# Grouped MoE on one core: the conditional of the rare pass moves from the second pair to the first, its loads change queue, and a nested conditional is taken out of its parent

## The chip, the core and the metric

The kernel runs on one core of a Trainium2 chip. The metric is the time of one execution on the device in microseconds (us), the median of several runs. TensorE (PE in the profile) multiplies matrices, ScalarE (ACT) evaluates functions, VectorE (DVE) does elementwise work, GpSimd (POOL) a little, and SyncE (SP) issues the loads. Each engine runs its own list of instructions in order and waits for others by semaphores.

## What is computed

The reference is a hybrid block followed by a two-layer block, 256 tokens of width 1024, in float32. The change lies in the second one:

```python
for l in range(2):
    h = rmsnorm(x, norm1_g[l]) * (1.0 + sc1) + sh1
    x = x + g1 * token_mix(h, ...)          # HGRN2 and latent attention
    h = rmsnorm(x, norm2_g[l]) * (1.0 + sc2) + sh2
    x = x + g2 * grouped_moe(h, w_router, router_bias, w_gate[l], w_up[l], w_down[l])
...
for e in range(N_EXPERTS):                  # in grouped_moe: 16 experts, top 2 of one group
    he = jax.nn.silu(t @ w_gate[e]) * (t @ w_up[e])
    y = y + combine[:, e:e + 1] * (he @ w_down[e])
```

A token goes to two experts, so `combine` is mostly zero, and the kernel computes an expert for its own tokens only. How many these are is known at run time alone.

## The kernel before

**Loads.** All weights are read as pages of 1 MB ([128, 2048] in float32) in the order of a list, PLAN. `pump` (L322) issues the next loads as long as a buffer is free, all from SyncE's queue (L346); `get` hands a page out and `release` (L377) gives buffers back and calls `pump`. Since SyncE's list is in order, a load issued behind something that waits, waits with it. In the MoE a pair of experts takes 12 pages (8 of gate and up, 4 of down), and 16 buffers are there. In layer 0 w166 is the first load that needs a buffer of pair 0; w174 to w181 hold gate and up of pair 2, w182 to w185 its down weights.

**The MoE** (`moe`, L1757) works on eight pairs of experts. Two pairs are fixed, the other six are sorted by load, so that their pages are found by indices in registers. For each pair: `gate_up` of slots 0 to 31 of both experts (L1593, 32 groups of matmuls over four blocks of partitions); `more_gate_up` (L1633), which holds a conditional for slots 32 to 63 (`If(cv > 32)`, L1637) and inside it, for the pairs with a limit of 96, one for slots 64 to 95 (`If(cv > 64)`, L1650); the release of 8 pages; the part of the previous pair's scatter for slots over 64 (L1773); `slot_w` (L1521), which sums the slots' weights; the scatter of the previous pair back to the tokens in two halves (L1532, L1533); `swiglu` (L1601 transposes, L1605 Silu on ScalarE, L1606 product on VectorE); and `downs` (L1657), which multiplies by the down weights (L1615) and copies the result (L1541, L1542). After every second pair `gather` (L1474) fetches the tokens of the next two pairs by a one-hot matmul (L1483), which ScalarE and VectorE copy into page tiles (L1490, L1492); the same pool of page tiles, from `self.page()`, serves several users. The next `gate_up` reads these tiles.

**The rare pass** (`rest`, L1744) computes what doesn't fit the limits: an outer conditional on the largest load, `If(top > NORMAL)` (L1749, NORMAL is 96), and in it sixteen inner ones (L1753) around `rare` (L1681). In this input no expert has over 96 tokens, so the outer one is skipped in both layers. Its body stands in the lists of four engines (PE, ACT, DVE, SP). `RARE_AT` names the pair at which it is placed, behind that pair's `swiglu`. The loads of `rare` fill page tiles from SyncE's queue (L1708).

**Order.** The instructions are placed on each engine by a scheduler that follows priorities; `issue_after` holds what is in it behind a named instruction. An `If` becomes a branch on every engine named. On an engine that skips it, a short row of instructions stands behind the branch, which waits for and adds to semaphores so that the counts are as if the body had run.

Of the kernel before, what the change touches and what calls it, by code (L numbers as in the profile page):

```python
# [11 lines left out]
F32 = mybir.dt.float32  # L12
# [3 lines left out]
AF = mybir.ActivationFunctionType  # L16
ALU = mybir.AluOpType
AX = mybir.AxisListType
ENG = mybir.EngineType

P = 128
S = 256
D = 1024
# [4 lines left out]
NPAIR = 8  # L28
# [184 lines left out]
FIXED = 2  # L213
NDYN = NPAIR - FIXED
# [1 line left out]
LIMITS = tuple([96] * FIXED + [96 if r < 3 else 64 for r in RANKS])  # L216
NORMAL = 96
HALF = 64
RARE_AT = 1
LEVELS = (64, 32, 16, 8, 4, 2, 1, 0)  # L220


# [52 lines left out]
class K:  # L275
# [71 lines left out]
            self.tiles[i] = t  # L347
            self.owner[i] = own

    def weight(self, i):  # L350
        if i not in self.dyn:
            return self.d["w"][i]
        return self.d["w"][bass.ds(self.dyn[i], 1)].rearrange("a p c -> p (a c)")

    def extra(self, pool, n, keys, cut=0):
        i = self.taken
# [1276 lines left out]
    def more_gate_up(self, p, cv, gu, x1, tg, h2, pw):  # L1633
        nc, tc = self.nc, self.tc
        ox = self.rt.tile([P, 2, S], F32, name=self.uid("ox"), tag="ox")
        more = LIMITS[p] > HALF
        with tc.If(cv > 32):  # L1637
            if more:
                xs = self.over_pick(p, 64)
            ps = self.mm()  # L1640
            last = self.gate_up(ps, gu, x1, range(4))
            if more:
                last = self.chain(last, self.over_turn(xs, ox))
            self.weigh(pw, p, 0, 1)
            last = self.gate_up(ps, gu, x1, range(4, 8), last)
            nc.scalar.activation(tg, ps, AF.Copy)
            if not more:
                return
            with tc.issue_after(last.ins):
                with tc.If(cv > 64):  # L1650
                    ps = self.mm()
                    self.gate_up(ps, gu, lambda k, e: ox[:, k // 4, (k % 4) * 64 + 32 * e:(k % 4) * 64 + 32 * e + 32])
                    t2 = self.sq512()
                    nc.scalar.activation(t2, ps, AF.Copy)
                    self.swiglu(t2, h2)

    def downs(self, p, cv, dn, hT, y, w, more):  # L1657
        nc, tc = self.nc, self.tc
# [22 lines left out]
    def rare(self, p, e, lo, w0):  # L1681
        nc = self.nc
        v = nc.vector
        c = [tt * 16 + 2 * p + e for tt in range(2)]
        pos = self.small(2)
        for tt in range(2):
            src = self.posm[:, c[tt]:c[tt] + 1]
            v.scalar_tensor_tensor(pos[:, tt:tt + 1], src, float(lo), src, ALU.is_gt, ALU.mult)
        o = min(lo, P)
        io = self.co("iota")[:, o:o + P]  # L1690
        pm = self.tmp.tile([P, 2, P], F32R, name=self.uid("pm"), tag="t1")
        for tt in range(2):
            v.tensor_scalar(pm[:, tt], io, pos[:, tt:tt + 1], None, ALU.is_equal)
        xo = []
        for h in range(2):
            ps = self.pick(pm, h)
            xs = self.sq512()
            nc.scalar.activation(xs, ps, AF.Copy)
            pt = self.acc()
            for i in range(4):  # L1700
                nc.tensor.transpose(pt[:, i * P:(i + 1) * P], xs[:, i * P:(i + 1) * P], self.ident)
            x = self.sq512()
            self.modulated(x[:, :], pt[:, :].rearrange("p (k s) -> p k s", k=4), h, P)
            xo.append(x)

        def load(i, half):
            t = self.page()
            nc.sync.dma_start(out=t, in_=self.weight(w0 + 12 * p + i)[:, half * 1024:(half + 1) * 1024])  # L1708
            return t

        gps = [self.acc() for _ in range(2)]
        for h in range(2):
            for u in range(2):
                for half in range(2):
                    t = load(4 * h + 2 * u + e, half)
                    for k2 in range(2):
                        k = 2 * half + k2
                        nc.tensor.matmul(gps[u], lhsT=xo[h][:, k * P:(k + 1) * P], rhs=t[:, k2 * 512:(k2 + 1) * 512],
                                         start=(h == 0 and k == 0), stop=(h == 1 and k == 3))
        sg = self.sq512()  # L1720
        nc.scalar.activation(sg, gps[0], AF.Silu)
        v.tensor_tensor(sg, sg, gps[1], ALU.mult)
        pt = self.acc()
        for f in range(4):
            nc.tensor.transpose(pt[:, f * P:(f + 1) * P], sg[:, f * P:(f + 1) * P], self.ident)
        hT = self.sq512()
        nc.scalar.activation(hT, pt, AF.Copy)
        pw = self.tmp.tile([P, 2, P], F32, name=self.uid("pw"), tag="t1")
        for tt in range(2):
            v.tensor_scalar(pw[:, tt], io, pos[:, tt:tt + 1], self.comb[:, c[tt]:c[tt] + 1], ALU.is_equal, ALU.mult)  # L1730
        w, st = self.slots()
        self.slot_w(pw, w, st)
        pss = [self.acc() for _ in range(2)]
        for f in range(4):
            t = load(8 + 2 * (f // 2) + e, f % 2)
            for n in range(2):
                nc.tensor.matmul(pss[n], lhsT=hT[:, f * P:(f + 1) * P], rhs=t[:, n * 512:(n + 1) * 512],
                                 start=(f == 0), stop=(f == 3))
        for n in range(2):
            yh, yl = self.sq512(F32R), self.sq512(F32R)  # L1740
            self.y_out(yh, yl, pss[n], w)
            self.scatter(yh, yl, st, 4 * n, 4)

    def rest(self, w0):  # L1744
        engs = [ENG.PE, ENG.Activation, ENG.DVE, ENG.SP]
        load = lambda i: self.count(i, engs)
        top = self.nc.values_load(self.srti[0:1, 2 * NDYN:2 * NDYN + 1], engines=engs, min_val=0,
                                  max_val=S + NORMAL - HALF)
        with self.tc.If(top > NORMAL):  # L1749
            for p in range(NPAIR):  # L1750
                cv = load(p)
                for lo in (LIMITS[p], LIMITS[p] + P):
                    with self.tc.If(cv > lo):  # L1753
                        for e in range(2):
                            self.rare(p, e, lo, w0)

    def moe(self, l, ahead):  # L1757
# [7 lines left out]
        tg = [self.rt.tile([P, 512], F32, name=self.uid("tg"), tag=f"tg{i}") for i in range(2)]  # L1765
        nc.gpsimd.memset(tg[1], 0.0)
        xe = self.gather(self.pm0)
        prev = cvp = None
        more = [self.rt.tile([P, D], F32R, name=self.uid("y2"), tag=f"y2{i}") for i in range(2)]
        more += self.slots("st2")  # L1770
# [5 lines left out]
        for p in range(NPAIR):  # L1776
            base = (p % 2) * P
            pw = self.rt.tile([P, 2, P], F32, name=self.uid("pw"), tag="pw")
            self.weigh(pw, p, 0)
            gu = [[[self.get(nm) for _ in range(2)] for nm in ("w_gate_2", "w_up_2")] for _ in range(2)]  # L1780
            x = lambda lvl: lambda k, e: xe[k // 4][:, (k % 4) * S + base + 64 * e + 32 * lvl:
                                                    (k % 4) * S + base + 64 * e + 32 * lvl + 32]
            hT = [self.rt.tile([P, S], F32, name=self.uid("hT"), tag=f"hT{i}") for i in range(3)]
            ps = self.mm()
            last = self.gate_up(ps, gu, x(0))
            nc.scalar.activation(tg[0], ps, AF.Copy)
            cv = self.count(p, engs)
            with self.tc.issue_after(last.ins):
                self.more_gate_up(p, cv, gu, x(1), tg[1], hT[2], pw)
            gu = None  # L1790
            self.release(8)
            if p > 0 and LIMITS[p - 1] > HALF:
                more_scatter()
            w, st = self.slots("sT", 2)
            self.slot_w(pw, w, st)
            last = None
            if prev is not None:
                self.scatter(*prev, 0, 4)
            for i in range(2):
                self.swiglu(tg[i], hT[i])  # L1800
            if p == RARE_AT:
                self.rest(w0)
            if prev is not None:
                last = self.scatter(*prev, 4, 4, 512)
            if p % 2 == 1 and p < NPAIR - 1:
                xe = self.gather(self.onehot(p // 2 + 1)[0])
            dn = [[self.get("w_down_2") for _ in range(2)] for _ in range(2)]
            if p == NPAIR - 1:
                ahead()
            y = [self.pga.tile([P, D], F32R, name=self.uid("pg"), tag="pg") for _ in range(2)]  # L1810
            with ExitStack() as after:
                if last is not None:
                    after.enter_context(self.tc.issue_after(last.ins))
                self.downs(p, cv, dn, hT, y, w, more)
            prev, cvp = (y[0], y[1], st), cv
            dn = None
            self.release(4)
# [213 lines left out]
```

## Time and profile before

| | before |
|---|---|
| median of 3 runs | 1503.02 us (1501.43 to 1504.09) |
| profiled execution | 1502.92 us |
| its span in the trace | 1501.1 us |
| mean granted clock of TensorE | 0.959 |
| TensorE busy | 1367.6 us (91%) |
| VectorE busy | 969.4 us (65%) |
| ScalarE busy | 680.7 us (45%) |
| read and written in device memory | 401.7 MB, 268 GB/s over the span |

The span is the time from the first to the last instruction that the trace holds; the execution's own time is 1.8 us longer. The two token mixes of the second block stand at 505 to 738 and 996 to 1229 us, the two MoEs behind them. In the rows of the trace, the us in brackets are the time that the engine sat idle before that group, and the name behind the arrow is what ended it. A name with a q (PEq, SPq) stands for an engine's sequencer, which takes branches, semaphores and the issue of transfers. "PEld" is the load of a matmul's stationary operand.

### The profile page before, as it was taken

The page shows a single profiled execution, that of the slowest core. Times are in us where ns is not written, and L with a number is a line of the kernel's source. Part 1 is how long each engine was busy: PE and PEld are TensorE (multiplying, and loading weights), DVE is VectorE, ACT ScalarE, POOL GpSimd, SP SyncE. Part 2 cuts the span into 40 slices and gives each one's busy share as a digit, 9 for nine tenths or more (in the row PEclk, how much of TensorE's full clock was granted, in tenths as well). Part 3 has the DMA queues.
Part 4 walks back from the last instruction along what each step waited for, and adds up shares of the span by engine and source line. Part 5 has one row for each costly group of instructions (what it writes and reads, how often), then busy time and mean ns, then how long its engine had stood idle before and what let it go on. Part 6 is the DMA issues. An engine that isn't in the chain of part 4 may idle for free. (4 is left out here: it accounts for less than half of the span.)

```text
span 1501.1 us, 27480 instructions
## 1 busy us (share of the span) xinstructions
PE 1367.6 (91%) x10654; PEld 1090.7 (73%) x10654; DVE 969.4 (65%) x2157; ACT 680.7 (45%) x1464; POOL 72.6 (5%) x86
## 2 busy tenths in 40 slices
PE   7999999989999999999856899988999986689988
PEld 7999998879999987999723344368789982334424
DVE  7999677888888788986621334368888762133323
ACT  7565458665556577555311112247756532011212
POOL 2010000010000003000100000000200010000010
PEclk9999999999999999999987999999999998799998
DMA  9787425368787143496687789963339678868895
GB/s 377 307 326 296 156 100 177 131 273 331 293 332 275 45 147 122 191 383 219 274 362 315 311 363 379 421 244 128 141 155 379 232 301 325 352 270 350 346 420 214
DMA packets 56904, 403.99 MB, mean 269 GB/s; under 512 B 6432, under 2 KB 6560, under 8 KB 8992
## 3 DMA queue, kind: packets, MB, share of 16 engines
q1 hardware_dynamic: 56736, 401.74, 67.6%
q8 instruction: 107, 1.75, 0.5%
q14 instruction: 61, 0.50, 0.1%
HBM read 400.66 MB, written 1.05 MB: 268 GB/s over the span
## 5 line engine op out<-in xcount | busy, mean ns | idle before, releaser
L389 ACT ACTIVATE whi<-w 128x512 fp32r<-128x512 f32 (+3 forms) x438 | 309.0, 737 | 242.7 <-PE mm L407 143.3
L390 DVE TENSOR_TENSOR wlo<-w,whi 128x512 fp32r<-128x512 f32 (+3 forms) x438 | 354.4, 829 | 62.0 <-ACT whi L389 60.4
L406 PE MATMUL mm<-nh,whi 128*128 128x256 f32 x1312 | 373.4, 285 | 14.3 <-ACT whi L389 13.5
L408 PE MATMUL mm<-nh,wlo 128*128 128x256 f32 x1312 | 370.8, 283 | 4.8 <-DVE wlo L390 4.8
L407 PE MATMUL mm<-nl,whi 128*128 128x256 f32 x1312 | 370.1, 282 | 0.3 <-DVE nl L529 0.2
L406 PEld LDWEIGHTS mm<-nh,whi 128*128 128x128 f32 x1312 | 249.7, 190 | 16.6 <-ACT whi L389 14.1
L408 PEld LDWEIGHTS mm<-nh,wlo 128*128 128x128 f32 x1312 | 249.2, 190 | 7.1 <-DVE wlo L390 6.5
L407 PEld LDWEIGHTS mm<-nl,whi 128*128 128x128 f32 x1312 | 249.8, 190 | 1.8 <-DVE nl L529 0.7
L1593 PE MATMUL mm<-w,pg 128*32 128x512 f32 x1472 | 184.5, 616 | 27.2 <-ACT pg L1490 19.6
L1593 PEld LDWEIGHTS mm<-w,pg 128*32 128x32 f32 x1472 | 51.1, 113 | 145.8 <-issue 104.6
L499 DVE SCALAR_TENSOR_TENSOR ada<-w,cact,ada 128x512 f32<-128x512 f32 x168 | 128.3, 763 | 6.5 <-ACT ada L496 3.6
L406 PE MATMUL acc<-hh,whi 128*128 128x256 f32 x352 | 98.9, 283 | 1.0 <-ACT whi L389 1.0
L407 PE MATMUL acc<-hl,whi 128*128 128x256 f32 x352 | 99.1, 282 | 0.0
L408 PE MATMUL acc<-hh,wlo 128*128 128x256 f32 x352 | 99.1, 283 | 0.0
L1536 DVE SCALAR_TENSOR_TENSOR xTt<-acc,mod,xTt 128x256 f32<-128x256 f32 x152 | 64.1, 475 | 38.2 <-PE acc L1533 38.0
L406 PEld LDWEIGHTS acc<-hh,whi 128*128 128x128 f32 x352 | 66.8, 190 | 1.1 <-ACT whi L389 1.1
L407 PEld LDWEIGHTS acc<-hl,whi 128*128 128x128 f32 x352 | 67.0, 190 | 0.0
L408 PEld LDWEIGHTS acc<-hh,wlo 128*128 128x128 f32 x352 | 67.0, 191 | 0.0
L1542 DVE SCALAR_TENSOR_TENSOR pg<-mm,sm,pg 128x512 fp32r<-128x512 f32 x32 | 23.8, 750 | 57.7 <-ACT pg L1541 46.6
L407 PE MATMUL mm<-wlo,nh 128*128 128x512 f32 (+2 forms) x144 | 54.8, 381 | 5.1 <-DVE wlo L390 5.1
L1510 DVE TENSOR_TENSOR pw<-cot,posp 128x128 f32<-128x128 f32 x52 | 12.9, 286 | 70.3 <-PE acc L1521 70.2
L1490 ACT ACTIVATE pg<-acc,mod,sm 128x256 f32<-128x256 f32 x32 | 17.4, 564 | 87.3 <-SPq L1749 60.1
(424 smaller groups left out, 2334.5 us busy)
## 6 DMA issues: line engine op xcount, KB each, us to landing
w<-in_w_dram SPq DMA_DIRECT2D x371, 1024.0 KB, 8.7
w<-in_w_dram SPq DMA_DIRECT2D x4, 832.0 KB, 8.3
w<-in_w_dram SPq DMA_DIRECT2D x4, 576.0 KB, 3.7
xTt<-in_xT_dram SPq DMA_DIRECT2D x2, 512.0 KB, 6.0
w<-in_w_dram SPq DMA_DIRECT2D x2, 512.0 KB, 7.3
mT<-in_memT_dram SPq DMA_DIRECT2D x1, 1024.0 KB, 17.4
bias<-in_alibi_dram SPq DMA_DIRECT2D x1, 1024.0 KB, 4.7
out_dram<-nl SPq DMA_DIRECT2D x4, 256.0 KB, 3.1
```

The lines of the kernel that those rows point to most:

```text
L389: a = self.nc.scalar.activation(hi[:, c], ap[:, c], AF.Copy)
L390: d = self.nc.vector.tensor_tensor(lo[:, c], ap[:, c], hi[:, c].bitcast(F32), ALU.subtract)
L406: mm(ps, lhsT=l[0], rhs=r[0], start=start, stop=False)
L407: mm(ps, lhsT=l[0], rhs=r[1], start=False, stop=False)
L408: mm(ps, lhsT=l[1], rhs=r[0], start=False, stop=stop)
L499: nc.vector.scalar_tensor_tensor(a, raw[:, k * 512:(k + 1) * 512], self.cact[:, 4 * h + k:4 * h + k + 1], a, ALU.mult, ALU.add)
L1490: nc.scalar.activation(o, ps[:, :S], AF.Identity, bias=sh, scale=g)
L1510: self.nc.vector.tensor_tensor(p4, io, b4(self.posm), ALU.is_equal)
L1536: nc.vector.scalar_tensor_tensor(self.xT[:, k], ps[:, i * S:(i + 1) * S], self.mod[:, self.l, 40 + k:41 + k], self.xT[:, k], ALU.mult, ALU ...
L1542: self.nc.vector.scalar_tensor_tensor(yl, ps, w, yh.bitcast(F32), ALU.mult, ALU.subtract)
L1593: last = self.chain(last, self.nc.tensor.matmul(ps[32 * g:32 * g + 32, :], lhsT=x(k, e), rhs=gu[k // 4][w][e][:, (k % 4) * 512:(k % 4 + 1) ...
```

## The change

It does four things. (1) `RARE_AT` goes from 1 to 0, and the call of `rest` moves into the `issue_after` right behind `more_gate_up`, ahead of the release of that pair's pages, `slot_w` and `swiglu`. (2) The loads in `rare` go to tiles of their own ("rp") and are issued from ScalarE's queue, with page indices in ScalarE's registers. (3) A Silu of four columns is added behind the first gather, whose result nobody reads. (4) The conditional for slots 64 to 95 stands behind the one for slots 32 to 63 instead of in it.

```diff
-RARE_AT = 1
+RARE_AT = 0
...
-    def weight(self, i):
-        if i not in self.dyn:
+    def weight(self, i, dyn=None):
+        dyn = self.dyn if dyn is None else dyn
+        if i not in dyn:
             return self.d["w"][i]
-        return self.d["w"][bass.ds(self.dyn[i], 1)].rearrange("a p c -> p (a c)")
+        return self.d["w"][bass.ds(dyn[i], 1)].rearrange("a p c -> p (a c)")
...
             nc.scalar.activation(tg, ps, AF.Copy)
-            if not more:
-                return
-            with tc.issue_after(last.ins):
-                with tc.If(cv > 64):
-                    ps = self.mm()
-                    self.gate_up(ps, gu, lambda k, e: ox[...])
-                    t2 = self.sq512()
-                    nc.scalar.activation(t2, ps, AF.Copy)
-                    self.swiglu(t2, h2)
+        if not more:
+            return
+        with tc.If(cv > 64):
+            ps = self.mm()
+            self.gate_up(ps, gu, lambda k, e: ox[...])
+            t2 = self.sq512()
+            nc.scalar.activation(t2, ps, AF.Copy)
+            self.swiglu(t2, h2)
...
         def load(i, half):
-            t = self.page()
-            nc.sync.dma_start(out=t, in_=self.weight(w0 + 12 * p + i)[:, half * 1024:(half + 1) * 1024])
+            t = self.rt.tile([P, D], F32, name=self.uid("rp"), tag="rp")
+            nc.scalar.dma_start(out=t, in_=self.weight(w0 + 12 * p + i, self.rdyn)[:, half * 1024:(half + 1) * 1024])
             return t
...
                     with self.tc.If(cv > lo):
+                        self.rdyn = {}
+                        if p >= FIXED:
+                            q = p - FIXED
+                            r = self.nc.values_load(self.srti[0:1, NDYN + q:NDYN + q + 1], engines=[ENG.Activation], ...)
+                            self.rdyn = {w0 + 12 * p + i: r + i for i in range(12)}
...
         xe = self.gather(self.pm0)
+        nc.scalar.activation(self.small(4), self.sp8, AF.Silu)
...
                 self.more_gate_up(p, cv, gu, x(1), tg[1], hT[2], pw)
+                if p == RARE_AT:
+                    self.rest(w0)
             gu = None
             self.release(8)
...
-            if p == RARE_AT:
-                self.rest(w0)
```

Lines behind the changed ones are numbered 1 higher in the changed kernel from L350 on, and 6 to 9 higher from L1757 on, so that L1593 is L1594 there; L1749 stays L1749.

**SyncE, layer 0, around the branch of the rare pass.** `w...` are the weight loads, `cnti` the counts, L1463 (L1464 in the changed kernel) reads a count into a register. Before:

```order
L346 DMA w183_9857<-in_w_dram 128x2048
L346 ISA
L346 DMA w184_9859<-in_w_dram 128x2048
L346 ISA
L346 DMA w185_9861<-in_w_dram 128x2048
L1749 COMPARE_AND_BRANCH
L1463 TENSOR_LOAD cnti_1202_9213
L1753 COMPARE_AND_BRANCH
L1708 DMA pg_1302_9996<-in_w_dram 128x1024
L1708 DMA pg_1303_10000<-in_w_dram 128x1024
```

And in the changed kernel:

```order
L1638 UNCONDITIONAL_BRANCH
L1650 UNCONDITIONAL_BRANCH
L346 DMA w166_14437<-in_w_dram 128x2048
L1749 COMPARE_AND_BRANCH
L1464 TENSOR_LOAD cnti_1202_9213
L1753 COMPARE_AND_BRANCH
L1753 UNCONDITIONAL_BRANCH x2
L1753 COMPARE_AND_BRANCH
```

The branch moved from behind w185 to behind w166, ahead of 19 loads, and its body on SyncE holds no load any more.

**TensorE, layer 0, the branch of the rare pass.** `cot` is the identity for transposes, `sT` the slot matrix of a scatter, `ox` the tokens of slots 64 to 95. Before, in pair 1:

```order
L1601 MATMUL acc_9914<-cot,tg_9325 128x128 x4
L1601 MATMUL acc_9922<-cot,tg_9326 128x128 x4
L1747 TENSOR_LOAD srti_9263
L1749 COMPARE_AND_BRANCH
L1463 TENSOR_LOAD cnti_9213
L1753 COMPARE_AND_BRANCH
```

In the changed kernel, in pair 0:

```order
L1594 MATMUL mm_9500<-w_8814,ox_9434 32x512
L1602 MATMUL acc_9535<-cot,sq_9533 128x128 x4
L1650 UNCONDITIONAL_BRANCH x2
L1747 TENSOR_LOAD srti_9263
L1749 COMPARE_AND_BRANCH
L1464 TENSOR_LOAD cnti_9213
```

The branch moved from between the transposes and the second half of a scatter in pair 1 to the place right behind the conditional for slots 64 to 95 in pair 0; 1448 rows of the list lie between it and its end (L1749 UNCONDITIONAL_BRANCH).

**ScalarE, layer 0, in the token mix.** `whi` is the rounded part of a weight page, `ga` a tile of gates. The changed kernel:

```order
L390 ACTIVATE whi_7073<-w_6746 128x512 x2
L1774 ACT_TABLE_LOAD
L1774 ACTIVATE sm_9374<-sp_676 128x4
L1070 ACTIVATE ga_6820<-acc_6824,smt 128x128
...
L1145 ACTIVATE pg_7202<-acc_7245 96x512
L390 ACTIVATE whi_7646<-w_7005 128x512
L944 ACT_TABLE_LOAD
L944 ACTIVATE pg_7257<-pg_7257 128x1024
```

The small Silu (L1774) and its table load stand there, some 200 rows ahead of the MoE; before, the same place has no table load, one stands at L1130 between the two parts shown, and none at L943. In the MoE both lists have a table load at L1786 (L1793) and one at L1605 (L1606) in pair 0.

## Rows read from the trace of the kernel before

**Rows 1.** Page, total and part 1: engine, busy us (share) xinstructions.

```profile
span 1501.1 us, 27480 instructions
...
PE 1367.6 (91%) x10654; PEld 1090.7 (73%) x10654; DVE 969.4 (65%) x2157; ACT 680.7 (45%) x1464; POOL 72.6 (5%) x86
```

**Rows 2.** TensorE's timeline, 745 to 830: start, us, line, op [idle before <-releaser].

```profile
754.17 0.41 PE L1521 MATMUL acc<-cot,pw 128*128 128x128 f32 x2 [0.33 <-PEq L1637]
...
759.03 5.34 PE L1615 MATMUL mm<-w,hT 128*32 128x512 f32 x32 [2.96 <-DVE hT L1606]
764.16 7.22 PE L1593 MATMUL mm<-w,pg 128*32 128x512 f32 x64
775.53 0.41 PE L1521 MATMUL acc<-cot,pw 128*128 128x128 f32 x2 [4.15 <-PEq L1773]
...
785.28 0.55 PE L1532 MATMUL acc<-sT,pg 128*128 128x256 f32 x1 [6.61 <-DVEq L1749]
...
796.52 3.64 PE L1615 MATMUL mm<-w,hT 128*32 128x512 f32 x32 [0.55 <-issue]
809.87 10.04 PE L1593 MATMUL mm<-w,pg 128*32 128x512 f32 x66 [9.71 <-ACT pg L1490]
819.85 0.50 PE L1562 MATMUL acc<-nh,pm 128*128 128x512 f32 x1
...
821.88 3.63 PE L1593 MATMUL mm<-w,pg 128*32 128x512 f32 x30
```

**Rows 3.** Line L1749: op xcount, ns min/median/max, first and last start; then who waited.

```profile
L1749 SPq EVENT_SEMAPHORE  x18: 17/17/17, 793.6 to 1300.7; - x18
...
L1749 PEldq COMPARE_BRANCH  x2: 6151/6328/6506, 778.0 to 1269.1; - x2
...
L1749 SPq COMPARE_BRANCH  x2: 53/53/53, 788.3 to 1279.4; - x2
...
  ACT pg L1490: 60.1, 2
```

**Rows 4.** Line L346 at the issue of w166, then at that of w181.

```profile
L346 SPq DMA_DIRECT2D w<-in_w_dram x1: 337/337/337, 754.1 to 754.1; - x1
...
DMA to landing us min/median/max: 4.8/4.8/4.8
...
L346 SPq DMA_DIRECT2D w<-in_w_dram x1: 332/332/332, 777.7 to 777.7; - x1
...
DMA to landing us min/median/max: 21.3/21.3/21.3
```

**Rows 5.** Windows: us, busy (xcount) by engine, granted clock, DMA share, GB/s.

```profile
760.00:770.00 10.00, 10.00 (x84) 4.20 (x80) 1.50 (x2) 1.37 (x2) 0.00 (x0) 0.85 1.01 424
810.00:820.00 10.00, 10.00 (x67) 2.47 (x67) 5.04 (x14) 2.34 (x5) 0.00 (x0) 0.79 0.92 367
820.00:830.00 10.00, 10.00 (x82) 3.89 (x86) 1.42 (x4) 1.18 (x2) 0.00 (x0) 1.00 0.14 56
920.00:990.00 70.00, 67.02 (x533) 29.94 (x526) 28.45 (x72) 15.05 (x33) 0.00 (x0) 1.00 0.98 401
```

**Rows 6.** SyncE's waits, 735 to 1000: us in total, times, longest.

```profile
SPq L346 <- PE mm L1593: 39.2, 4, 21.0
```

**Rows 7.** TensorE's waits in layer 1's MoE, 1229 to 1500: total, times, longest.

```profile
PE mm L1593 <- ACT pg L1490: 9.9, 1, 9.9
...
PE mm L1593 <- DMA w<-in_w_dram: 5.8, 3, 3.9
```

**Rows 8.** ScalarE's timeline in the token mix of layer 0, 545 to 580.

```profile
549.68 2.75 ACT L1069 ACTIVATE ga<-acc,smt 128x128 fp32r<-128x128 f32 x10 [4.08 <-PE acc L1065]
...
558.03 1.28 ACT L1130 ACT_TABLE_LOAD   x1
```

**Rows 9.** Windows: the token mix of layer 0 as one stretch.

```profile
505.00:738.00 233.00, 222.45 (x1703) 207.96 (x1702) 187.02 (x429) 141.90 (x337) 20.09 (x20) 0.99 0.56 215
```

**Rows 10.** Line L1650: who waited for it (us, times).

```profile
  PE acc L1521: 1.8, 3
```

More of the change, by code (lines that the diff above doesn't have):

```diff
@@ L1646, in more_gate_up @@
             nc.scalar.activation(tg, ps, AF.Copy)
-            if not more:
-                return
-            with tc.issue_after(last.ins):
-                with tc.If(cv > 64):
-                    ps = self.mm()
-                    self.gate_up(ps, gu, lambda k, e: ox[:, k // 4, (k % 4) * 64 + 32 * e:(k % 4) * 64 + 32 * e + 32])
-                    t2 = self.sq512()
-                    nc.scalar.activation(t2, ps, AF.Copy)
-                    self.swiglu(t2, h2)
+        if not more:
+            return
+        with tc.If(cv > 64):
+            ps = self.mm()
+            self.gate_up(ps, gu, lambda k, e: ox[:, k // 4, (k % 4) * 64 + 32 * e:(k % 4) * 64 + 32 * e + 32])
+            t2 = self.sq512()
+            nc.scalar.activation(t2, ps, AF.Copy)
+            self.swiglu(t2, h2)
     def downs(self, p, cv, dn, hT, y, w, more):
@@ L1753, in rest @@
                     with self.tc.If(cv > lo):
+                        self.rdyn = {}
+                        if p >= FIXED:
+                            q = p - FIXED
+                            r = self.nc.values_load(self.srti[0:1, NDYN + q:NDYN + q + 1], engines=[ENG.Activation],
+                                                    min_val=w0, max_val=w0 + 12 * NPAIR - 12)
+                            self.rdyn = {w0 + 12 * p + i: r + i for i in range(12)}
                         for e in range(2):
```

## The prediction

> **What bounds the kernel now.** I read the page's totals first, then TensorE's timeline at the start of the first layer's MoE, then what waits at the conditional of the rare pass, then the weight loads, and last the same stretch of the second layer. The totals [rows 1] show TensorE busy for 1367.6 of 1501.1 us: a change off its chain earns nothing, and 133.5 us of idle time are all there is to win. TensorE's timeline [rows 2] shows where a block of that idle time lies. In pair 0 it waits 0.33 us at the skip of L1637 and 2.96 us for VectorE's product ahead of the down matmuls; in pair 1 4.15 us behind the skipped conditionals, 6.61 us at the rare pass's conditional (L1749); in pair 2 9.71 us before the first gate/up matmul, and this matmul waits for ScalarE's gathered tokens (L1490). Behind that, the timeline runs on with small gaps.
>
> Line L1749 by itself [rows 3] explains the two long ones. TensorE's branch over the rare pass lasts 6.15 and 6.51 us in the two layers, so the engine stands though nothing is computed. SyncE takes the same branch at 788.3 and sends its first event at 793.6. ScalarE's gather then waits 60.1 us in two occurrences, 30 us a layer, for SyncE's events from this line. The cause is in the program: the rare pass's body writes the page tiles that the gather uses also, from SyncE's queue, and a skipped body has to report as if it had been done. In the order of before, SyncE reaches that branch only behind the 20 loads w166 to w185, and it passes the branch when these have landed. The loads [rows 4] show when: w166 is issued at 754.1 and lands 4.8 us later, w181 is issued at 777.7 and lands 21.3 us later, at 799.0. Meanwhile the queue moves 424 GB/s [rows 5], 1.05 MB in 2.47 us. Four more loads follow w181, so the last lands near 799.0 + 4 x 2.47 = 808.9, and at 809.87 pair 2 starts. All this recurs in layer 1, where the wait for the gather is 9.9 us [rows 7].
>
> **The change part by part.** *SyncE's branch moves to pair 0.* It now stands behind w166 alone. w166 lands at 754.1 + 4.8 = 758.9; the code fetch that the branch seems to cost, 793.6 - 788.3 = 5.3 us [rows 3], runs beside this and ends at about 759.6 at the latest. w167, until now issued right behind w166, is issued at some 759.1 and lands 4.8 us later at 763.9. Today it follows w166 in the stream, at about 758.9 + 2.5 to 3 = 761.9. So the stream behind is some 2 us late: w181 lands at 801.0. If branch and landing followed one another instead of overlapping, it would be 806; that end is kept for the range. In return, the restart of the queue at 809 goes.
>
> *The gather's wait goes.* In the changed kernel the rare pass loads into a tile of its own from ScalarE's queue, so no page of the gather hangs on SyncE. The gather is then bound by TensorE and ScalarE alone. What is late next is the load of pair 2's gate/up weights, w174 to w181: the second half of its matmuls needs the last four.
>
> *TensorE's branch moves to pair 0.* The timeline shows no branch of this size there. The bounds: the 0.33 us of the skip at that place [rows 2], and the 6.61 us of the same branch a pair later. I take 5, nearer to the second, since the body jumped over is the same, while the load stream beside it is thinner. That delays pair 0 by 4.7 us (0 to 6.3): the down matmuls start at 759.03 + 4.7 = 763.7, pair 1's gate/up at 764.16 + 4.7 = 768.9 and it ends 7.2 later, at 776.1. Behind it I take the 0.33 us of a cheap skip instead of 4.15, and keep 4.15 as the other end: slot_w starts about 0.4 later, at 776.5. From slot_w to L1749 TensorE took 785.28 - 6.61 - 775.53 = 3.1 us, and from there to the down matmuls 796.52 - 785.28 = 11.2: these start at 791, end 3.64 later at 794.6, and the first half of pair 2's gate/up follows until 798 or 800. Then it waits for w181, at 801.0. So the two chains nearly meet, and the load ends last: the 5 us that I chose are covered by it up to 1 us more or so, and each us beyond that costs one.
>
> *The end of pair 2's gate/up.* Half of it takes 3.6 us at full speed (30 matmuls, 821.88) and 10.04 - 3.6 = 6.4 us in the run behind the 9.71 us gap [rows 2]. [...] I take 6, as TensorE has idled again before this half. With 0.3 allowed between landing and first matmul, 801.0 + 0.3 + 6 = 807.3, where the next step (L1562) starts at 819.85 today. The gain is 12.5 us a layer. With the fast half it is 15; with w181 at 806 and the slow half it is 7.1.
>
> *Does it last to the end?* Behind pair 2 TensorE is busy 67.02 of 70 us and the loads fill 0.98 of the time in 920 to 990 [rows 5], so either could take something back. But the stream had room before: between 820 and 830 it was busy for 0.14, as no buffer was free; SyncE waited 21.0 us for TensorE's gate/up to give one back [rows 6]. The four loads issued from 809.85 on land by 809.85 + 4.8 + 3 x 2.47 = 822.1; the next is issued 21 us behind them, so it lands at some 837.5, 15.4 later instead of 2.5. These 12.9 us are the room. Buffers come free through TensorE's own progress, so the loads move with it, and 12.5 fits. I let the gain last. Layer 1 alone has 5.8 us of waits on loads at L1593 [rows 7], which move with the stream.
>
> *The early Silu.* The listing shows that it isn't where the diff has it: it is put into the token mix, ahead of L1069's copies, where ScalarE waits 4.08 us today [rows 8]. One table load (1.28 us) that stood at 558.03 goes there and costs nothing; another appears ahead of the Exp (L943), on an engine busy for 141.90 of 233 us [rows 9]. In the MoE the two loads at pair 0 stay. So the Silu wins nothing. What else it does is to re-order pieces of the token mix on three engines. TensorE is busy for 222.45 of those 233 us; I put this at 0, with 3 us a layer either way.
>
> *The block for slots 64 to 95 out of its parent.* It adds a branch where both are skipped, in pairs 0 and 1, where the loads cover it. The later three skips of L1650 exist today and cost 1.8 us together [rows 10]. In the pairs that execute it, the first copy comes a little earlier: under 1 us each. I put it at 0.
>
> **Sum.** 1502.92 (this execution, whose span is 1501.1) - 2 x 12.5 = 1477.9. The execution lies 0.1 below the median of 1503.02, so the forecast against the median is 1478.0.
>
> **The rivals.** *Code waits bind (A).* All branches could cost what the dear ones do, so that TensorE's chain, and not the load, ends last: pair 0 late by 6.3, pair 1 with two skips of 4.15. Pair 1's gate/up ends at 777.7, slot_w starts at 786.0, down at 786.0 + 14.3 = 800.3, pair 2 at 803.9, and with the slow 10.04 it ends at 813.9: a gain of 5.9, so 1502.9 - 11.8 = 1491. For it speaks that the skips behind pair 0's and pair 1's gate/up cost 0.33 and 4.15 [rows 2], so the price hangs on where code lies; against it, that the body under one skip is now cut in two short ones. [...]
>
> *The loads take it back (B).* If the late pairs are bound by the stream and it can't start earlier by more than half of what TensorE gains, 6.2 us a layer remain: 1490.5. For it: the 0.98 and the 5.8 us; against: the slack at 820.
>
> *The token mix pays (C).* The re-ordered pieces stand in TensorE's in-order queue; where one comes ahead of its input, everything behind it waits. The point from which this decides is 12.5 + 1.5 = 14 us a layer, more than the 10.5 us of idle time that TensorE has in all of 505 to 738 [rows 9]; idle time there would have to more than double. At 15 us a layer the time is 1502.9 - 25 + 30 = 1508, slower. Against it: each piece is only moved by a few places, and ScalarE has 91 us free there.
>
> **How the numbers follow.** The forecast has 0.70, A 0.10, B 0.08, C 0.06, and 0.06 go to a gain beyond the fast end, below 1469, or to other smaller gains. A measurement of this kernel can tell 0.2%, 3 us, from no change. Faster: 0.90; within: 0.04, for a gain eaten nearly whole; slower: 0.06. The range reaches from 1469 (15 us twice and the token mix 2 us better each: 1502.9 - 34) to 1492, which takes in A and B.
>
> **What would show it.** In the changed profile SyncE passes L1749 near 759 and no load stops behind w185; TensorE's first matmul behind L1749 comes near 759 in pair 0; the 9.71 us wait on ScalarE's gather is replaced by a wait on a load (w181), of some 1 to 6 us, inside pair 2's gate/up; L1562 starts near 807. It is wrong if pair 2 still waits on the gather; if TensorE reaches pair 2 behind 801; if the stretch from 505 to 738 changes by over 3 us; or if the last pairs show new waits on loads.

## The result and the profile after

| | before | changed |
|---|---|---|
| median | 1503.55 us (4 runs, 1501.43 to 1504.72) | 1478.79 us (4 runs, 1475.23 to 1480.86) |
| ratio | | 0.9834, 95% interval 0.981 to 0.9859 |
| profiled execution (span) | 1502.92 (1501.1) | 1477.15 (1475.4) |

The kernel is 1.7% faster, and the forecast of 1478.0 is 0.8 us off the median. The two profiled executions differ by 25.8 us. Before asking how far the forecast's parts were right, here is where the time went. I cut TensorE's timeline of both traces at the first gate/up matmul of pair 0, at the first matmul of L1562 (L1563) in pair 2, and at the last down matmul of pair 7:

| us | before | changed | difference |
|---|---|---|---|
| layer 0: pair 0 to pair 2 | 73.1 | 58.9 | -14.2 |
| layer 0: pair 2 to the end of pair 7 | 170.1 | 167.0 | -3.1 |
| layer 1: pair 0 to pair 2 | 73.2 | 59.2 | -14.0 |
| layer 1: pair 2 to the end of pair 7 | 173.9 | 172.1 | -1.8 |
| all ahead of the two MoEs | 995.0 | 1002.3 | +7.3 |

So the MoEs gave 33.1 us and the stretches ahead of them took 7.3 back. TensorE's timeline at the start of layer 0's MoE, which answers to [rows 2] (columns as there; lines are numbered one higher):

```profile
749.64 7.07 PE L1594 MATMUL mm<-w,pg 128*32 128x512 f32 x64
764.75 0.66 PE L1522 MATMUL acc<-cot,pw 128*128 128x128 f32 x2 [8.03 <-PEq L1749]
...
769.75 5.07 PE L1616 MATMUL mm<-w,hT 128*32 128x512 f32 x32 [2.63 <-DVE hT L1607]
774.63 7.74 PE L1594 MATMUL mm<-w,pg 128*32 128x512 f32 x64
783.53 0.41 PE L1522 MATMUL acc<-cot,pw 128*128 128x128 f32 x2 [1.17 <-PEq L1780]
...
793.95 3.64 PE L1616 MATMUL mm<-w,hT 128*32 128x512 f32 x32 [2.15 <-issue]
797.38 4.46 PE L1594 MATMUL mm<-w,pg 128*32 128x512 f32 x34
802.49 1.05 PE L1594 MATMUL mm<-w,pg 128*32 128x512 f32 x4 [0.66 <-DMA w<-in_w_dram]
804.97 3.63 PE L1594 MATMUL mm<-w,pg 128*32 128x512 f32 x28 [1.43 <-DMA w<-in_w_dram]
808.53 0.50 PE L1563 MATMUL acc<-nh,pm 128*128 128x512 f32 x1
```

The 9.71 us wait for the gather is gone, as are the 6.61 and 4.15 us of pair 1. In their place stand 8.03 us at the branch in pair 0, and 0.66 and 1.43 us for loads within pair 2's gate/up. The line of the branch, which answers to [rows 3] (op xcount, duration in ns min/median/max, first and last start, then who waited, us and times):

```profile
L1749 SPq EVENT_SEMAPHORE  x18: 17/17/17, 759.1 to 1242.6; - x18
...
L1749 ACTq COMPARE_BRANCH  x2: 45/45/45, 752.5 to 1231.1; - x2
...
L1749 SPq COMPARE_BRANCH  x2: 50/52/53, 757.9 to 1236.5; - x2
L1749 PEldq COMPARE_BRANCH  x2: 6291/6662/7032, 758.0 to 1236.6; - x2
...
  PE acc L1522: 16.9, 2
```

SyncE now takes the branch at 757.9 and has its first event at 759.1. TensorE's branch lasts 6.29 and 7.03 us. ScalarE takes it at 752.5, ahead of the end of the gate/up matmuls, and no gather waits for the line. The loads of w166, w167 and w181, each at its issue, answer to [rows 4]:

```profile
L346 SPq DMA_DIRECT2D w<-in_w_dram x1: 337/337/337, 757.5 to 757.5; - x1
...
DMA to landing us min/median/max: 5.6/5.6/5.6
...
L346 SPq DMA_DIRECT2D w<-in_w_dram x1: 328/328/328, 763.8 to 763.8; - x1
...
DMA to landing us min/median/max: 6.0/6.0/6.0
...
L346 SPq DMA_DIRECT2D w<-in_w_dram x1: 333/333/333, 784.8 to 784.8; - x1
...
DMA to landing us min/median/max: 20.1/20.1/20.1
```

w166 lands at 763.1, w167 at 769.8 and w181 at 784.8 + 20.1 = 804.9, just when the last 28 matmuls of pair 2's gate/up begin (804.97). Layer 1 runs alike: 8.82 us at the branch, and one wait of 0.49 us for a load ahead of the same 28 matmuls.

### The profile page after: what moved, and what is told of

The parts are those of the page before. It is cut to its first block, busy times and chain, and to the rows that moved or that the text cites. A ratio compares the mean times of both kernels' runs of the same rounds, so it can differ in the third digit from the quotient of the medians.

```text
span 1475.4 us, 27498 instructions
## 1 busy us (share of the span) xinstructions
PE 1359.5 (92%) x10654; PEld 1083.0 (73%) x10654; DVE 966.2 (65%) x2157; ACT 685.4 (46%) x1468; POOL 77.8 (5%) x86
## 5 line engine op out<-in xcount | busy, mean ns | idle before, releaser
L407 PE MATMUL mm<-nh,whi 128*128 128x256 f32 x1312 | 373.4, 285 | 14.2 <-ACT whi L390 13.5
L1594 PE MATMUL mm<-w,pg 128*32 128x512 f32 x1472 | 181.2, 602 | 11.7 <-DMA w<-in_w_dram 9.3
L1594 PEld LDWEIGHTS mm<-w,pg 128*32 128x32 f32 x1472 | 50.0, 111 | 127.4 <-issue 105.5
L1537 DVE SCALAR_TENSOR_TENSOR xTt<-acc,mod,xTt 128x256 f32<-128x256 f32 x152 | 63.7, 476 | 17.6 <-PE acc L1534 17.3
L1542 ACT ACTIVATE pg<-mm,sm 128x512 fp32r<-128x512 f32 x32 | 22.0, 687 | 80.4 <-PE mm L1628 40.6
```

The lines of the kernel that those rows point to most:

```text
L407: mm(ps, lhsT=l[0], rhs=r[0], start=start, stop=False)
L1537: nc.vector.scalar_tensor_tensor(self.xT[:, k], ps[:, i * S:(i + 1) * S], self.mod[:, self.l, 40 + k:41 + k], self.xT[:, k], ALU.mult, ALU ...
L1542: self.nc.scalar.activation(yh, ps, AF.Copy, scale=w)
L1594: last = self.chain(last, self.nc.tensor.matmul(ps[32 * g:32 * g + 32, :], lhsT=x(k, e), rhs=gu[k // 4][w][e][:, (k % 4) * 512:(k % 4 + 1) ...
```

## The experiments

All ratios are against the kernel before. Beside the medians, which hold all that varies from run to run, I use the sum of the two MoEs in each profile, from the first gate/up matmul of pair 0 to the end of pair 7's down matmuls (before: 243.2 + 247.1 = 490.3; changed: 225.9 + 231.3 = 457.2), and the rest ahead of them (995.0 and 1002.3). There is one profile of each kernel, and differences of 1 to 2 us between two profiles are not told apart from chance.

| kernel | ratio (95%) | median us | MoEs | ahead of them |
|---|---|---|---|---|
| changed | 0.9834 (0.981 to 0.9859) | 1478.79 | 457.2 | 1002.3 |
| e1 changed, no Silu | 0.9782 (0.9762 to 0.9801) | 1470.88 | 458.2 | 995.0 |
| e2 before, Silu only | 1.0054 (1.0036 to 1.0073) | 1511.4 | 489.3 | 998.8 |
| e3 changed, nested again | 0.9854 (0.9826 to 0.9881) | 1480.93 | 461.7 | 1001.6 |
| e4 before, un-nested only | 1.0004 (0.9988 to 1.002) | 1503.54 | 492.1 | 991.3 |
| e5 before, tile and ScalarE's queue | 0.9809 (0.9789 to 0.983) | 1475.93 | 464.4 | 997.1 |
| e6 changed, no rare pass | 0.9853 (0.9826 to 0.988) | 1479.66 | 453.2 | 1005.8 |
| e7 e1, conditional behind swiglu | 0.9816 (0.9793 to 0.9839) | 1474.86 | 459.3 | 992.6 |
| e8 e1, GpSimd's queue | 0.98 (0.9775 to 0.9826) | 1473.94 | 460.3 | 997.4 |
| e9 before, tile only | 0.9828 (0.9809 to 0.9846) | 1475.62 | 465.0 | 993.2 |
| e10 changed, SyncE's queue | 0.9823 (0.9802 to 0.9843) | 1475.98 | 457.1 | 1007.0 |
| e11 e1, conditional at pair 5 | 0.9855 (0.9838 to 0.9873) | 1480.13 | 467.2 | 997.1 |
| e12 e5 and un-nested | 0.9847 (0.9826 to 0.9867) | 1477.86 | 462.4 | 996.0 |

### Which part won it: tile, queue or place

**e9** takes the smallest piece of the change alone: the rare pass's loads get a tile of their own, and nothing moves.

```diff
         def load(i, half):
-            t = self.page()
+            t = self.rt.tile([P, D], F32, name=self.uid("rp"), tag="rp")
             nc.sync.dma_start(out=t, ...)
```

> The kernel before with a tile of its own for the rare pass's loads, but still from SyncE's queue and in pair 1, so that SyncE reaches its branch behind w185 as before. Theory (the gather waited for the shared page tiles only): the 9.7 us wait is gone, TensorE goes from pair 1's down straight to pair 2, SyncE's restart behind w185 delays w186 to w189, which pair 3 needs late: 1476 to 1480, as with ScalarE's queue. Rival (the queue is what counts, as SyncE's stop behind w185 holds pair 2's or pair 3's loads): 1490 to 1503.

The theory held: 1475.62, just below the 1476 expected, and a ratio of 0.9828, which the interval of the whole change covers. SyncE still stands at its branch behind w185, and in layer 0 issues no load from 790.9 to 813.0 (the line of the branch in this kernel):

```profile
L1749 SPq EVENT_SEMAPHORE  x18: 17/17/17, 796.7 to 1287.6; - x18
...
L1749 SPq COMPARE_BRANCH  x2: 53/53/53, 791.3 to 1267.8; - x2
```

ScalarE's gather (L1490 in layer 0: its instructions, then what ended its idle time) waits for TensorE only:

```profile
L1490 ACT ACTIVATE pg<-acc,mod,sm x16: 564/565/567, 745.0 to 931.9; 128x256 f32<-128x256 f32 x16
...
  PE acc L1483: 28.5, 16
```

and TensorE's timeline goes from pair 1's down matmuls at 800.17 to pair 2's gate/up at 803.60 without a gap, while the 6.57 us at the branch stay:

```profile
789.44 0.55 PE L1532 MATMUL acc<-sT,pg 128*128 128x256 f32 x1 [6.57 <-DVEq L1749]
...
800.17 3.64 PE L1615 MATMUL mm<-w,hT 128*32 128x512 f32 x32 [0.62 <-issue]
803.60 7.89 PE L1593 MATMUL mm<-w,pg 128*32 128x512 f32 x66
811.42 0.50 PE L1562 MATMUL acc<-nh,pm 128*128 128x512 f32 x1
```

Of the 33.1 us that the MoEs gain in the whole change, this one line gives 25.3.

**e5** adds ScalarE's queue, with the page indices read into ScalarE's registers as in the change; the conditional stays in pair 1. Against e9 the edit is:

```diff
-            nc.sync.dma_start(out=t, in_=self.weight(w0 + 12 * p + i)[...])
+            nc.scalar.dma_start(out=t, in_=self.weight(w0 + 12 * p + i, self.rdyn)[...])
...
```

> The kernel before with the rare pass's loads on ScalarE's queue and in a tile of their own, the conditional staying in pair 1. Theory (the 9.7 and 9.9 us before pair 2 hang on the page tiles alone): that wait goes, TensorE's 6.6 us at the branch and SyncE's stop behind w185 stay, and the time falls by 2 x 9.7 to about 1484. Rival (SyncE's stop itself holds pair 2, through its loads): 1502.

0.9809 and 1475.93, better than the 1484 that I expected. Some 4 of these 8 us come from pair 2, which runs its gate/up in 7.9 us instead of 10.0 when no gap stands ahead of it, and 2 more lie behind pair 2. On SyncE the branch isn't where I expected it: it stands behind w172, with the loads held from 760.0 to 777.5 in layer 0, and no longer behind w185. So e5 differs from e9 in the queue and in that place. The two together add nothing that can be told: 464.4 and 465.0 in the MoEs.

**e10** is the other half of that question: the whole change, with the loads back on SyncE.

```diff
-            nc.scalar.dma_start(out=t, in_=self.weight(w0 + 12 * p + i, self.rdyn)[...])
+            nc.sync.dma_start(out=t, in_=self.weight(w0 + 12 * p + i)[...])
...
```

> The changed kernel with the rare pass's loads back on SyncE's queue, in their own tile, at pair 0. Theory (SyncE then jumps over a body of some 700 rows, whose code fetch of 5.3 us comes on top of the landing of w166 or runs beside it; only if it comes on top is the load stream later): beside it, 1479; on top, up to 5 us a layer more, 1489. It tells what the other queue is worth once the tile is free.

457.1 us in the MoEs against 457.2: SyncE's longer body costs nothing there. In layer 0 its first event comes 5.8 us behind its branch instead of 1.2 (762.3 to 768.1), but w166 lands only at 767.4, so the time runs beside the landing. Once the tile is free, the queue doesn't matter for this input.

**e12** is the change without the move and the Silu (e5 with the diff's un-nested block).

> The kernel before with ScalarE's queue, the own tile and the un-nested block, the conditional still in pair 1, no Silu: all of the change without the move and the Silu. Theory (the un-nesting wins 1 to 1.2 us a layer behind pair 2, the move of the conditional wins the rest up to 1470.9): 1473.5. Rival (the un-nesting wins nothing that is kept, as alone): 1476.

The median is 1477.86, above both values expected, and its interval overlaps that of e5. The MoEs' 462.4 against 464.4 are the theory's size, but behind pair 2, where the theory has it, only layer 0 is shorter (1.3 us). From here to e1 only the move of the conditional is left: on TensorE, ScalarE and VectorE from pair 1 to pair 0, on SyncE from behind w172, where it stands as in e5, to behind w166. The MoEs go from 462.4 to 458.2, and the ratio from 0.9847 to 0.9782. So the move wins some 4 us in the MoEs, nearly all between pair 0 and pair 2 (61.0 and 60.9 to 58.9 and 59.1); the medians differ by more, which I don't explain.

### What the early Silu cost

**e1** takes the line out of the changed kernel, **e2** puts it alone into the kernel before.

```diff
         xe = self.gather(self.pm0)
-        nc.scalar.activation(self.small(4), self.sp8, AF.Silu)
```

> The changed kernel without the early Silu of four columns. Its token mix stands in the order of before. Theory (the Silu and the order that it brings cost the token mix what it lost, 2.0 us in layer 0 and 4.5 in layer 1, and the first gather another 0.9 in layer 0): the time falls from 1478.8 to about 1472, and the stretch between the last down matmuls of layer 0 and the mask matmul (L1381 or L1382) of layer 1 is 243.6 us again instead of 248.1. Rival (the token mix is only shifted against the loads, and the moved conditional is what changed it): 1478.8 and 248.

> The kernel before, with only the early Silu added. Theory: all of the token mix's loss comes with it and nothing in the MoE is won, so 1503.5 + 6.5 = 1510, with both table loads of pair 0 still there. Rival (the Silu helps the MoE, as a table that is already there would save 1.28 us a layer): 1503.5 - 2.6 = 1501.

Both theories held in the times: 1470.88, and 1511.4. From the end of layer 0's pair 7 to layer 1's first gate/up matmul e1 takes 247.1 us, the changed kernel 252.7 and the kernel before 248.2. e2's profile, the shortest of its six runs, has 248.2 there, so what it shows of the loss (3.8 us) lies ahead of layer 0's MoE. The MoEs stay where they were (458.2 and 489.3), so the Silu helps nothing there. Of the 14 profiles of this study, the five with the Silu need 1003.1 us ahead of the MoEs on the mean (998.8 to 1007.0), the nine without 995.0 (991.3 to 997.4). ScalarE's timeline in the changed kernel shows the two table loads, the second of them new:

```profile
546.07 1.28 ACT L1774 ACT_TABLE_LOAD   x1
...
576.17 1.28 ACT L944 ACT_TABLE_LOAD   x1
```

and TensorE's waits between 570 and 650 (us in total, times, longest) show what the order does, in the changed kernel and then in e1:

```profile
PE acc L650 <- ACT pT L647: 3.0, 1, 3.0
PE acc L645 <- ACT pg L944: 2.2, 1, 2.2
...
PE acc L645 <- DVE pr L643: 0.4, 1, 0.4
```

```profile
PE acc L645 <- DVE pr L643: 2.3, 4, 1.1
```

Four waits of 2.3 us in sum became three of 5.6 behind ScalarE's Exp (L944) and the transposes' copies (L647). This is layer 0; in layer 1's token mix the waits at these two lines grow from 2.3 to 4.5 us in the same way. So these waits account for 5.5 of some 8 us, and the rest stays open.

### The nested block

**e3** nests the block again in the changed kernel, **e4** un-nests it alone in the kernel before.

```diff
-        if not more:
-            return
-        with tc.If(cv > 64):
+            if not more:
+                return
+            with tc.issue_after(last.ins):
+                with tc.If(cv > 64):
```

> The changed kernel with the block for slots 64 to 95 nested again. Theory (the 3.1 us that layer 0 won behind pair 2, 2.2 of them between the middles of pairs 2 and 4, come from the un-nesting: pairs 2 and 4 of layer 0 and pair 2 of layer 1 execute the block): slower by about 4, 1483. [...]

> The kernel before with only the block for slots 64 to 95 taken out. Theory (1 us or so for each of the three executed blocks, and the 4.15 us wait behind pair 1's two skips becomes short; but in pair 1 everything waits for SyncE anyway, so only the first part is kept): 1503.5 - 3 = 1500.5. Rival (two skips in a row cost more than one jump): 1503.5 to 1505.

e4 shows no difference (1.0004), and e3 (0.9854 against 0.9834) none that the intervals tell. By stretch, the part of e3 behind pair 2 is 1.0 longer in layer 0 and 0.5 shorter in layer 1 than in the changed kernel; in e4 it is 1.4 longer in layer 0 than before. The 4.5 us by which e3's MoEs are longer come nearly all from layer 0 between pair 0 and pair 2 (63.7 against 58.9; layer 1 has 58.4 against 59.2). There w168 and w169 land 4.5 and 4.0 us behind their forerunners (2.5 and 2.7 in the changed kernel), and the last 28 matmuls of pair 2's gate/up, behind longer waits for loads, take 6.25 us instead of 3.63; one profile doesn't tell whether the nesting did that. My theory of 4 us for the block is not borne out, and no gain is shown. Nor does it shorten the 4.15 us behind pair 1's skips: they are 4.12 in e4 and 4.09 in e12, un-nested both, and 0.74 in e3 and 1.17 in the changed kernel, where the conditional of the rare pass has left pair 1.

### What the conditional still costs, and where it should stand

**e6** leaves the rare pass out.

```diff
-                if p == RARE_AT:
-                    self.rest(w0)
```

> The changed kernel without the rare pass: its conditional and all in it are left out, so more than 96 tokens of an expert would not be computed. It prices what the conditional still costs. Theory (the 8.0 and 8.8 us of TensorE's wait in pair 0 and the 4.2 us that SyncE's stop adds to the load stream both go, after which the loads and TensorE meet again in pair 2): the stretch from pair 0's gate/up to L1563 of pair 2 falls from 58.9 to about 52.5 in both layers, 1466. Rival (only the load stream counts, so 4.2 a layer): 1470.

The median shows no gain (1479.66, with a profile that is 3.5 us longer ahead of the MoEs), and the MoEs only 4.0 us: 58.1 and 55.0 instead of 58.9 and 59.2 between pair 0 and pair 2, not 52.5. TensorE's waits in layer 0, 757 to 820, and its timeline at the end of pair 2's gate/up say why:

```profile
PE mm L1594 <- DMA w<-in_w_dram: 6.7, 3, 3.8
```

```profile
806.71 1.05 PE L1594 MATMUL mm<-w,pg 128*32 128x512 f32 x4 [3.84 <-DMA w<-in_w_dram]
809.21 6.35 PE L1594 MATMUL mm<-w,pg 128*32 128x512 f32 x28 [1.45 <-DMA w<-in_w_dram]
```

Without its 8 us at the branch TensorE is early in layer 0, and waits 6.7 us for pair 2's weights instead. From w166's issue to w181's landing 44.0 us pass there (765.2 to 809.2), 47.4 in the changed kernel, and TensorE's branch lies beside them. So what goes with the conditional is SyncE's stop: the last 28 matmuls start 51.8 and 51.4 us behind pair 0's first instead of 55.3 and 55.6, which is the rival's price (3.5 and 4.2). In layer 0 most of it is lost again, as these matmuls take 6.35 us instead of 3.63, at a granted clock of 0.56 (809.21 to 815.49), behind the waits of 3.84 and 1.45 us. The changed kernel, with 0.66 and 1.43 us, ran them at 1.00.

**e11** moves the conditional to pair 5 to see what it costs without this cover.

```diff
-RARE_AT = 0
+RARE_AT = 5
```

> The changed kernel without the early Silu, the conditional behind more_gate_up of pair 5 instead of pair 0. Theory (pair 0 hides most of the 8 us at the branch, because the 16 loads from w166 to w181 bound that stretch anyway; at pair 5 TensorE is the bound in layer 0, and in layer 1 its 7.3 us of waits on loads take the branch in): layer 0 gains 0.8 to 3 early and loses 6 to 8 late, layer 1 gains 3, 1473. Rival (the loads cover the branch there too): 1465.

Worse than both: 1480.13. The stretch up to pair 2 gets shorter, to 57.9 and 57.7, though in both layers its last 28 matmuls take the slow 6.52 and 6.35 us, behind waits of 3.81 and 3.33 us and a short one. Behind it 175.1 and 176.6 us stand against 168.7 and 171.6 in e1. The branch's wait has the same size in pair 5 of layer 0 (TensorE's timeline),

```profile
923.98 0.55 PE L1533 MATMUL acc<-sT,y 128*128 128x256 f32 x1 [8.05 <-PEq L1749]
```

and 6.4 us of it are paid. In layer 1 the later waits for loads at L1594 took in a part, falling from 5.9 us in e1 to 2.3, and still the stretch is 5.0 longer.

**e7** puts the conditional behind pair 0's swiglu.

```diff
-                if p == RARE_AT:
-                    self.rest(w0)
...
             for i in range(2):
                 self.swiglu(tg[i], hT[i])
+            if p == RARE_AT:
+                self.rest(w0)
```

> The changed kernel without the early Silu (1470.9 by the run above) and with the conditional behind pair 0's swiglu. Theory (TensorE's branch then runs beside the 2.6 us in which TensorE waits for the down matmuls' input, and SyncE passes its branch behind w173, with 8 loads under way, at the price of one restart of 2.3 us instead of 4.2): 2 to 2.6 us a layer, 1466. Rival (SyncE now has to wait for 8 landings, until 780, and the buffers that come free in between stay empty, so pair 2 is later): 1471 to 1478.

The MoEs take 459.3 us against 458.2, and the median of 1474.86 lies in the rival's range: no gain. SyncE's branch stands behind w167 in layer 0, not behind w173 as the theory had it. The branch's wait is now part of one of 13.88 us ahead of the down matmuls. Pair 2 starts at 798.55, 51.7 us behind pair 0's first matmul (48.7 in e1), and then runs without a wait for loads:

```profile
770.07 5.33 PE L1616 MATMUL mm<-w,hT 128*32 128x512 f32 x32 [13.88 <-issue]
...
798.55 7.89 PE L1594 MATMUL mm<-w,pg 128*32 128x512 f32 x66
```

**e8** has GpSimd issue the loads, so that SyncE has no branch there.

```diff
-            nc.scalar.dma_start(out=t, ...)
+            nc.gpsimd.dma_start(out=t, ...)
...
-        engs = [ENG.PE, ENG.Activation, ENG.DVE, ENG.SP]
+        engs = [ENG.PE, ENG.Activation, ENG.DVE, ENG.Pool]
...
```

> The changed kernel without the early Silu and with the rare pass's loads issued by GpSimd, so that GpSimd and not SyncE takes part in the conditional. Theory (SyncE's list then has no branch at L1749 and the load stream runs through: w181 lands 4.2 us earlier, and TensorE ends the stretch): 58.9 falls to about 56 in both layers, 1465. Rival (TensorE's own wait of 8 us is all that counts): 1470.9.

Half held: layer 0's stretch fell to 55.3 as expected, with no wait for a load left in pair 2's gate/up and TensorE's 8.1 us at the branch still there, so SyncE's stop alone costs 3.6 us in that layer. Layer 1's rose to 63.7. TensorE's waits in layer 1, 1218 to 1300, show where:

```profile
PE acc L1522 <- PEq L1749: 8.1, 1, 8.1
PE mm L1616 <- issue: 4.7, 3, 3.4
PE acc L1602 <- issue: 3.6, 1, 3.6
```

Behind the 8.1 us at the branch it stands another 3.6 and 4.7 us for which the profile shows nothing to wait for. Of the latter, a wait of 3.4 us ahead of the down matmuls stands in the changed kernel's layer 1 as well. What the others are, no run here shows.

## Why the prediction was right, point by point

**The main step was right, and one line of the diff carries it.** The gather's wait ended, as forecast, because the rare pass lost its hold on the page tiles: e9 alone gives 25.3 of the MoEs' 33.1 us. The prediction gave the end of this wait to tile and queue together, and had the restart of the loads at 809 go with the move; e9 and e10 show that the tile did it, and in e9 the restart is still there, at 813.0.

**The load stream as the next bound: right, with other terms.** I had w167 land 5.0 us behind w166; it landed 6.7 behind it. I had w181 land 801.0 - 746.8 = 54.2 us behind the first gate/up matmul of pair 0; it landed 804.9 - 749.6 = 55.3 behind it. The 5.3 us that I allowed SyncE at its branch, beside the landing, are not there in layer 0 (757.9 to 759.1); in layer 1 its first event comes 5.5 us behind the branch (1236.5 to 1242.0), beside a landing at 1241.7.

**TensorE's branch: sized wrong.** I took 5 and bounded it by 6.61; TensorE stood for 8.03 us in layer 0 and 8.8 in layer 1, and its first matmul behind L1749 came 15.1 us behind pair 0's first (764.75), not some 12. The place was right and so was the cover: e6 shows that the stretch gets only 0.8 and 4.2 us shorter without any branch, and that SyncE's stop, not TensorE's wait, is what it still costs. The branch itself lasts 6.29 and 7.03 us with the long body, where the short hops of pair 1 in layer 0 cost 1.17 us. That such time is a fetch of code, as I had it for the 5.3 us on SyncE, was my estimate. It fits that in the changed kernel 4 packets of the two queues that the profile lists as instruction queues (107 and 62 packets in the whole span) move during TensorE's branch in layer 0 and 6 in layer 1; which engine they are for, and whether it waits for them, the trace doesn't show. I had expected the branch to be cheaper in pair 0 for a thinner load stream beside it, and it wasn't.

**The second half of pair 2's gate/up: the slow one was taken, the fast one came.** I put it at 6 us, from the run behind a 9.71 us gap; with gaps of 0.66 and 1.43 us its last 28 matmuls took 3.63, at a granted clock of 1.00. The slow end exists: behind waits of 3.06 and 1.43 us in e3, and of 3.84 and 1.45 in e6, the same 28 took 6.25 and 6.35, at 0.57 and 0.56. So the size was right for a longer wait than the one that came. The prediction named the fast end as a gain of 15 a layer. From here, less the 1.1 us by which w181 is late, comes the stretch of 58.9 us instead of the forecast's 807.3 - 746.8 = 60.5.

**Behind pair 2 I forecast nothing, and 3.1 and 1.8 us came.** e12 against e5 gives 1.3 for the un-nesting in layer 0 (169.1 to 167.8, layer 1 equal), but e4 against before gives 1.4 the other way (170.1 to 171.5), and e1 takes 1.7 longer there than the changed kernel (168.7 against 167.0) with the same block. The gains are as large as such differences and stay open.

**The early Silu: the term that failed.** "I put this at 0, with 3 us a layer either way": so 6 us at the most, and it cost 7.9 by the medians of e1 and the changed kernel (1478.79 - 1470.88) and 8.1 by the mean stretch ahead of the MoEs in the profiles with and without it. What the prediction read from the listing, one table load more and no help in the MoE, was right; that ScalarE's free time would hide the rest wasn't, since TensorE's queue is in order and it was led to waits of 3.0 and 2.2 us.

**The sum was near for two reasons that cancel.** 25.0 us were forecast for the MoEs and 0 ahead of them; 33.1 and -7.3 came in the profile. That the total lies 0.8 us from the forecast is luck.

**The rivals.** A (TensorE's code waits bind) didn't occur: the branch cost more than its price there, but the two short skips of pair 1 cost 1.17 us together instead of 8.3, and the load ended last. The prediction held the shorter bodies against A; e3 and e4 show that it was the move that shortened this wait, not the un-nesting. That a skip's price hangs on where code lies was my estimate, from skips of 0.33 and 4.15 us; no run shows where it lies. B (the late loads take it back) didn't: in layer 1's MoE TensorE's waits on loads at L1594 rose only from 5.8 to 7.2 us:

```profile
PE mm L1594 <- DMA w<-in_w_dram: 7.2, 4, 3.8
```

C named the right place with the wrong size: some 4 us a layer, where 14 would have turned the sign.

**A faster version.** e1, the change without its Silu, is faster than both kernels: 0.9782 of before (0.9762 to 0.9801).

## What to carry to other kernels

A conditional that is never taken can still hold the tiles that its body writes (here 25.3 of 33.1 us): give its body buffers of its own before moving it about. Its branch has a price on the engines that take part (here 6 to 7 us on TensorE, and a stop of the loads on SyncE, 3.5 and 4.2 us by e6), which is hidden where a stretch waits for something else anyway, as e6 shows, and mostly paid elsewhere, as e11 shows (6.4 of 8.05 us in layer 0). Arriving early at a wait was not free here either: behind the longer waits the next 28 matmuls ran at a granted clock of 0.55 to 0.57 (e3, e6, e11) and took 2.6 to 2.9 us more. An instruction that depends on nothing is placed where the scheduler likes; read the listing for what it pushes aside, in all engines' queues, and don't put a re-ordering at nothing because the engine that it sits on has time.

## What was not expected of the hardware

The same token mix, in the same order, took 248.2 us in the kernel before and 243.5 in e4, from the end of pair 7 of layer 0 to layer 1's first gate/up. Windows of the two traces over nearly the same instructions (columns as in [rows 5]; 135 and 128 matmul records) differ in the granted clock. Before:

```profile
1020.00:1030.00 10.00, 8.70 (x48) 8.19 (x47) 7.33 (x13) 6.36 (x13) 1.79 (x3) 0.83 0.58 210
1030.00:1045.00 15.00, 12.79 (x87) 12.23 (x87) 12.11 (x36) 8.71 (x26) 0.00 (x0) 0.89 0.23 88
```

and e4:

```profile
1018.00:1028.00 10.00, 7.56 (x40) 6.49 (x39) 10.00 (x22) 8.28 (x18) 1.96 (x3) 1.00 0.35 102
1028.00:1041.00 13.00, 10.79 (x88) 10.21 (x87) 10.47 (x32) 8.94 (x23) 0.00 (x0) 1.00 0.49 192
```

Before, the granted clock is 0.83 and 0.89 on the mean; in e4 it is 1.00 in both windows. In both kernels TensorE had waited 4.0 us for ScalarE's `lp` (L986) ahead of it, so that wait alone doesn't decide; what does stays open. Cut at the same two matmuls, 62 records lie between 1022.62 and 1034.60 before (11.98 us, granted clock 0.87) and between 1024.07 and 1034.58 in e4 (10.51 us, 1.00): 1.5 of the 4.7 us. Such stretches may make up part of the spread of a few us between runs of one kernel, which no run here sizes; it is why small effects were read here from stretches of the MoE and not from whole times alone.
